# Two small unused tiles shift every SBUF pool of a one-core transformer layer

## The chip, the cores and the metric

The kernel runs on one core of a Trainium2 chip. The metric is the device time of one launch in microseconds; the kernel before has a median of 2428.5 us over three runs (2424.85, 2428.5 and 2429.57).

## The reference, cut to what matters

One layer of a hybrid backbone on 512 latent tokens (width 2048) with 256 context tokens in front of them, batch 1:

```
hx, hc = modulate(rms_norm(x)), modulate(rms_norm(ctx))      # scales and shifts from c @ w_mod, c_ctx @ w_mod
u, v, q, k, vv, g, d = split(hx @ w_in)                      # the same split of hc @ w_in for k, vv, d
a   = gelu(u) * (w_s @ layer_norm(gelu(v)) + b_s)            # chunks of 128 tokens, 8 heads
o   = gated linear attention of q, k, vv, d, forwards and backwards, starting from the context's state
y   = concat(a, norm(o) * silu(g)) @ w_out
x   = x + gate * rms_norm(y)
f   = (silu(h @ w_a) * (h @ w_b)) @ w_ffn_out                # h = modulate(rms_norm(x)), hidden width 5632
out = x + gate * rms_norm(f)
```

All inputs and the output are float32.

## The kernel before

**The products.** Each large product is built from TensorE matmuls of 128x128 weights against 512 streamed columns (256 for the context's keys). To keep float32 accuracy each operand is split in two float32r tiles: ScalarE copies the high part (`S.copy`), VectorE subtracts it from the source for the low part (`split`, L271; `parts`, L985). `three` (L295) then issues three matmuls for a pair, and L113 is the line of the helper `mm` that issues each:

```
        mm(o, a[0], b[0], start, False)
        mm(o, a[0], b[1], False, False)
        mm(o, a[1], b[0], False, stop)
```

The first operand is the stationary one (the weights that LDWEIGHTS puts in the array), the second the moving one, read column by column. The trace shows one LDWEIGHTS (PEld) for each matmul (PE). A small number of products (transposes by the identity, gate rows, the attention's small blocks) are in plain float32.

**The order.** Program order on each engine is the order of the code, fixed in advance. The stages are: the first modulation rows (`mb`), one third at a time of k, q and half of u (`k`, `q`, `u`), the rest of u and v (`u1a`, `v0a`, `v1a`), the context's keys and values (`ck` with its gate rows `cd`, then `cv`), the values and gates (`vv`, `g`) with the attention's small work threaded between, the output projection (`wo`), eleven groups of the FFN's input (`f0p` to `f10p`; each group computes 7 products of half size, 336 matmuls; `ffn_group`, L1133), the FFN's output in two halves (`fo`, L1241: 960 matmuls each) and its last four blocks of rows (`fz`, L1268: 192 matmuls). Weights come from DRAM through SyncE's queue in pieces of 512 KB.

**Where the tiles lie.** A tile pool takes a stretch of each partition's SBUF, from the left end upwards or (`side="right"`) from the right end downwards. A pool lies behind those that were opened before it. On the left stand, from byte 16512 of each partition: `cp` (constants and small vectors, 5856 bytes), `s2` (44 slots of 2 KB: the activations' split parts, called by `slot`), then `pp` with `sp`, `hcp` and `gl` one after the other, and later, in their place, `fp` (29 slots of 2 KB, by `fslot`). On the right stands `stg` (streamed weights, raw and split) and later, in its place, `st2` (the same for the second half of the kernel). The right end is at byte 229344.

Worked out from these sizes, the tiles of 2 KB of the left pools `s2`, `pp` and `fp` start at 2048 n + 1888, and the tiles of 2 and 4 KB of the right pools `stg` and `st2` at 2048 n + 2016. The context's tiles in `hcp` start at 2048 n + 864. Slices within a tile start at multiples of 512 bytes (128 columns of float32) further on, except for the gate rows' weights `wd`, whose slices step by 256 bytes. So, by the start modulo 512:

| matmuls | stationary operand | moving operand |
|---|---|---|
| `k`, `q`, `u`, `u1a`, `g` | right pool, 480 | `s2`, 352 |
| `v`, `vv`, `wo`, `f0p` to `f10p`, `fo` | `s2` or `fp`, 352 | right pool, 480 |
| `ck` | right pool, 480 | `hcp`, 352 |
| `cv` | `hcp`, 352 | right pool, 480 |
| `cd`, and `d` among `k` and `q` | `s2`, 352 and 96 in turn | `hcp` or `s2`, 352 |
| `fz` | `s2`, 352 | `s2` or `fp`, 352 |

All of these starts are 96 modulo 128.

Of the kernel before, what the change touches and what calls it, by code (L numbers as in the profile page):

```python
# [9 lines left out]
F32 = mybir.dt.float32  # L10
# [8 lines left out]
P = 128  # L19
# [72 lines left out]
def trunk_kernel(ctx, tc, cmat, cmask, x, c, ctxt, c_ctx, w_mod, b_mod, g_pre_mix, g_post_mix, g_pre_ffn,  # L92
# [4 lines left out]
    bg, bgm = Pump(), Pump()  # L97

    cp = ctx.enter_context(tc.tile_pool(name="cp", bufs=1))
    stg_ctx = ExitStack()  # L100
    stg = stg_ctx.enter_context(tc.tile_pool(name="stg", bufs=1, side="right"))
    s2 = ctx.enter_context(tc.tile_pool(name="s2", bufs=1))
# [1213 lines left out]
```

## Time and profile before

| | before |
|---|---|
| median of 3 runs | 2428.5 us |
| profiled execution | 2426.19 us, span 2424.4 us |
| PE busy (matmul) | 2319.1 us, 96% |
| PEld busy (weight load) | 1851.2 us, 76% |
| DVE / ACT / POOL busy | 1596.3 / 987.7 / 15.3 us |
| mean granted clock of TensorE | 0.979 |
| DMA | 470.99 MB, 194 GB/s over the span |

An engine's busy time is the time in which at least one of its instructions runs. Consecutive matmuls overlap in the records, so PE's busy share says only that it had work; how fast it goes is read from the starts of consecutive matmuls.

### The profile page before, as it was taken

To read this page: it belongs to the slowest core of one execution; us is meant where nothing else is said; L and a number is where in the kernel's file an instruction comes from. 1 tells how busy PE (TensorE), PEld (TensorE's weight loads), DVE (VectorE), ACT (ScalarE), POOL (GpSimd) and SP (SyncE) were. 2 spreads that over 40 slices of the span, in tenths; PEclk is the share of its full clock that TensorE was granted. 3 is DMA by queue.
4 is the path that set the end of the run, shared out by engine and by line. 5 is a ranking of instruction groups with operands and counts; after the bars stand their busy time and mean duration, and the time that the engine had idled before them with its cause. 6 is when DMAs were issued, how large, how long until landed. Compare 5 with 4: busy or idle time off the path is not lost.

```text
span 2424.4 us, 27761 instructions
## 1 busy us (share of the span) xinstructions
PE 2319.1 (96%) x10386; PEld 1851.2 (76%) x10386; DVE 1596.3 (66%) x2040; ACT 987.7 (41%) x1509; POOL 15.3 (1%) x22
## 2 busy tenths in 40 slices
PE   7999999999996989889999999999999899999998
PEld 2778888788885767658888778877787788888887
DVE  3876577677777777787778777877787632242246
ACT  4443234454564223854444444444344422241232
POOL 0000000000000000000000000000000000000000
PEclk9999998999997999899999999999999999999999
DMA  9957787734335989746567665765566542253344
GB/s 322 334 195 251 239 282 245 239 131 134 127 105 177 314 299 310 226 131 191 185 188 219 189 190 184 219 195 188 180 218 193 171 139 96 96 172 101 102 139 156
DMA packets 244134, 470.99 MB, mean 194 GB/s; under 512 B 20456, under 2 KB 31936, under 8 KB 244000
## 3 DMA queue, kind: packets, MB, share of 16 engines
q1 hardware_dynamic: 233280, 451.49, 57.6%
q10 hardware_dynamic: 10720, 17.74, 2.1%
q8 instruction: 81, 1.33, 0.2%
q14 instruction: 53, 0.43, 0.1%
HBM read 445.04 MB, written 24.13 MB: 194 GB/s over the span
## 4 chain that ended last, share of the span: by engine, by line
PE 81%; DMA 8%; DVE 6%; ACT 3%; issue 1%; SPq 0%; ACTq 0%; DVEq 0%
PE fo L113 19%; PE f7p L113 3%; PE f4p L113 3%; PE f9p L113 3%; PE f5p L113 3%; PE f1p L113 3%; PE f6p L113 3%; PE f3p L113 3%; PE f2p L113 3%; PE f10p L113 3%; PE f8p L113 2%; PE f0p L113 2%; PE v0a L113 2%; PE u1a L113 2%; PE g0a L113 2%; PE cv L113 2%
## 5 line engine op out<-in xcount | busy, mean ns | idle before, releaser
L1221 DVE TENSOR_TENSOR gl<-gr,gh 128x512 fp32r<-128x512 f32 x44 | 28.4, 687 | 24.2 <-ACT gh L1220 24.2
L1220 ACT CAST gh<-gr 128x512 fp32r<-128x512 f32 x44 | 25.1, 618 | 28.1 <-DMA gr<-g_dr 20.9
L226 DVE SCALAR_TENSOR_TENSOR m50acc<-m50w,cpair,m50acc 128x1024 f32<-128x1024 f32 x16 | 20.5, 1281 | 13.8 <-DMA m50w<-in_w_mod_dram 13.7
L990 DVE TENSOR_TENSOR fo_2l<-fo_r,fo_2h 128x1024 fp32r<-128x1024 f32 x8 | 9.8, 1226 | 29.6 <-ACT fo_2h L989 29.6
L829 ACT ACTIVATE lv<-lv 128x1024 f32<-128x1024 f32 x20 | 21.0, 1054 | 19.4 <-DVE lv L828 19.4
L990 DVE TENSOR_TENSOR fo_0l<-fo_r,fo_0h 128x1024 fp32r<-128x1024 f32 x8 | 9.8, 1225 | 28.3 <-ACT fo_0h L989 28.3
L113 PE MATMUL fo<-fo_0h,gh 128*128 128x512 f32 x64 | 26.4, 412 | 1.7 <-ACT gh L1220 1.7
L113 PE MATMUL vv0a<-vv_0h,hxh 128*128 128x512 f32 x64 | 27.7, 433 | 0.0
L990 DVE TENSOR_TENSOR fo_18l<-fo_r,fo_18h 128x1024 fp32r<-128x1024 f32 x8 | 9.8, 1225 | 27.1 <-ACT fo_18h L989 27.1
L990 DVE TENSOR_TENSOR fo_14l<-fo_r,fo_14h 128x1024 fp32r<-128x1024 f32 x8 | 9.8, 1225 | 26.3 <-ACT fo_14h L989 26.3
L113 PE MATMUL vv1a<-vv_0h,hxh 128*128 128x512 f32 x64 | 27.1, 424 | 0.0
L990 DVE TENSOR_TENSOR fo_12l<-fo_r,fo_12h 128x1024 fp32r<-128x1024 f32 x8 | 9.8, 1225 | 26.3 <-ACT fo_12h L989 26.3
L990 DVE TENSOR_TENSOR fo_10l<-fo_r,fo_10h 128x1024 fp32r<-128x1024 f32 x8 | 9.8, 1225 | 26.3 <-ACT fo_10h L989 26.3
L990 DVE TENSOR_TENSOR fo_16l<-fo_r,fo_16h 128x1024 fp32r<-128x1024 f32 x8 | 9.8, 1225 | 26.2 <-ACT fo_16h L989 26.2
L990 DVE TENSOR_TENSOR fo_8l<-fo_r,fo_8h 128x1024 fp32r<-128x1024 f32 x8 | 9.8, 1225 | 26.2 <-ACT fo_8h L989 26.2
L113 PE MATMUL g1a<-hxh,g_0h 128*128 128x512 f32 x64 | 26.6, 415 | 0.3 <-ACT g_0h L274 0.3
L113 PE MATMUL g0a<-hxh,g_0h 128*128 128x512 f32 x64 | 26.9, 420 | 0.0
L830 DVE TENSOR_TENSOR lv<-lv,kq 128x1024 f32<-128x1024 f32 x20 | 24.4, 1219 | 3.8 <-ACT lv L829 3.8
L113 PE MATMUL v1a<-v_0h,hxh 128*128 128x512 f32 x64 | 26.7, 417 | 0.0
L1280 ACT ACTIVATE junk<-fc 128x512 bf16<-128x512 f32 x16 | 10.1, 631 | 40.7 <-DVE fc L1279 40.6
L113 PEld LDWEIGHTS s<-lv 128*128 128x128 f32 x192 | 24.9, 191 | 2.0 <-issue 0.5
L113 PE MATMUL fo<-fo_0l,gh 128*128 128x512 f32 x64 | 26.0, 407 | 0.0
(3877 smaller groups left out, 8033.6 us busy)
## 6 DMA issues: line engine op xcount, KB each, us to landing
fo_r<-in_w_ffn_out_dram SPq DMA_DIRECT2D x80, 512.0 KB
gr<-g_dr SPq DMA_DIRECT2D x22, 512.0 KB
mx4w<-in_w_mod_dram SPq DMA_DIRECT2D x16, 512.0 KB
mx8w<-in_w_mod_dram SPq DMA_DIRECT2D x16, 512.0 KB
mx12w<-in_w_mod_dram SPq DMA_DIRECT2D x16, 512.0 KB
mc4w<-in_w_mod_dram SPq DMA_DIRECT2D x16, 512.0 KB
mc8w<-in_w_mod_dram SPq DMA_DIRECT2D x16, 512.0 KB
mc12w<-in_w_mod_dram SPq DMA_DIRECT2D x16, 512.0 KB
```

The lines of the kernel that those rows point to most:

```text
L113: return T.matmul(o, lhsT=l, rhs=r, start=start, stop=stop)
L226: ins = V.scalar_tensor_tensor(out=acc, in0=raw[:, j].rearrange("p i c -> p (i c)"), scalar=cvec[:, k0 + j:k0 + j + 1], in1=acc, op0=ALU.m ...
L829: S.activation(lv, lv, AF.Exp)
L830: V.tensor_tensor(out=lv, in0=lv, in1=kq[h], op=ALU.mult)
L990: V.tensor_tensor(out=wl, in0=src, in1=wh.bitcast(F32), op=ALU.subtract)
L1220: S.copy(hi, r[:, j * 512:(j + 1) * 512])
L1221: V.tensor_tensor(out=lo, in0=r[:, j * 512:(j + 1) * 512], in1=hi.bitcast(F32), op=ALU.subtract)
L1280: S.activation(junk, f, AF.Square, accum_out=fss[:, cg:cg + 1])
```

## The change

Two tiles are allocated and never used. `edge_l` (8 float32, 32 bytes of each partition) is the first tile of `cp` on the left, so everything on the left starts 32 bytes later. `edge_r` (24 float32, 96 bytes) stands in a pool of its own, opened on the right ahead of `stg`, so everything on the right starts 96 bytes earlier. No instruction is added, removed or moved.

```
     cp = ctx.enter_context(tc.tile_pool(name="cp", bufs=1))
+    edge = ctx.enter_context(tc.tile_pool(name="edge", bufs=1, side="right"))
+    edge.tile([P, 24], F32, name="edge_r")
+    cp.tile([P, 8], F32, name="edge_l")
     stg_ctx = ExitStack()
     stg = stg_ctx.enter_context(tc.tile_pool(name="stg", bufs=1, side="right"))
     s2 = ctx.enter_context(tc.tile_pool(name="s2", bufs=1))
```

After it, the tiles of `s2`, `pp` and `fp` start at 2048 n + 1920 and those of `stg` and `st2` too. Modulo 512 both columns of the table above read 384 (and the gate rows' weights 384 and 128), and every start in it is a multiple of 128. The constants' tile `mats` moves from a multiple of 128 to 32 past one.

## Rows read from the trace of the kernel before

**Rows 1.** The page: busy time by engine, and the chain that ended last.

```profile
PE 2319.1 (96%) x10386; PEld 1851.2 (76%) x10386; DVE 1596.3 (66%) x2040; ACT 987.7 (41%) x1509; POOL 15.3 (1%) x22
...
PE 81%; DMA 8%; DVE 6%; ACT 3%; issue 1%; SPq 0%; ACTq 0%; DVEq 0%
```

**Rows 2.** Windows by stage: busy us by engine, clock, DMA share, GB/s.

```profile
core 0: us, PE busy (x) PEld busy (x) DVE busy (x) ACT busy (x) POOL busy (x), PEclk, DMA share, GB/s
0.00:45.00 45.00, 29.66 (x77) 6.96 (x78) 13.31 (x66) 23.31 (x54) 3.81 (x10) 0.96 0.95 301
45.00:215.00 170.00, 165.16 (x743) 127.44 (x742) 124.83 (x189) 70.27 (x133) 0.96 (x1) 0.99 0.77 263
780.00:990.00 210.00, 194.28 (x801) 151.47 (x802) 152.04 (x152) 66.20 (x105) 2.87 (x3) 0.96 0.92 311
1107.00:1913.00 806.00, 803.46 (x3521) 645.46 (x3519) 621.12 (x621) 348.00 (x380) 0.00 (x0) 1.00 0.62 194
2149.00:2372.00 223.00, 223.00 (x962) 180.78 (x961) 78.04 (x85) 59.92 (x72) 0.00 (x0) 1.00 0.38 127
2372.00:2416.00 44.00, 43.71 (x193) 35.83 (x191) 30.82 (x60) 12.36 (x36) 0.00 (x0) 1.00 0.48 159
```

**Rows 3.** Who PE waited for in the FFN groups, 1107 to 1913 us.

```profile
PE f8p L113 <- DVE f8y2l L990: 0.4, 1, 0.4
PE f4T L1202 <- ACT f4t L1204: 0.2, 1, 0.2
```

**Rows 4.** Timeline of PE: first and last of the second half of `fo`.

```profile
2148.89 0.40 PE L113 MATMUL fo<-fo_0h,gh 128*128 128x512 f32 x1
...
2371.74 0.40 PE L113 MATMUL fo<-fo_18h,gl 128*128 128x512 f32 x1
```

**Rows 5.** Timeline of PE: the first, the 13th and the last of `fz`.

```profile
2371.98 0.40 PE L113 MATMUL fz<-flh,gh 128*128 128x512 f32 x1
...
2374.75 0.39 PE L113 MATMUL fz<-flh,gh 128*128 128x512 f32 x1
...
2415.33 0.39 PE L113 MATMUL fz<-flh,gl 128*128 128x512 f32 x1
```

**Rows 6.** Timeline of PE in `v0a`: first and last of 81 matmuls in a row.

```profile
286.23 0.40 PE L113 MATMUL v0a<-v_0l,hxh 128*128 128x512 f32 x1
...
304.90 0.40 PE L113 MATMUL v0a<-v_0h,hxh 128*128 128x512 f32 x1
```

**Rows 7.** Windows of PE around that stretch.

```profile
286.10:304.90 18.80, 18.80 (x82) 1.00 0.94 319
```

**Rows 8.** Timeline of PE in `u1a`: first and last of 131 matmuls in a row.

```profile
227.32 0.40 PE L113 MATMUL u1a<-hxh,u_0l 128*128 128x512 f32 x1
...
257.53 0.39 PE L113 MATMUL u1a<-hxh,u_0h 128*128 128x512 f32 x1
```

**Rows 9.** Timeline of PE: nine matmuls of `ck`, then nine of `cd`.

```profile
372.63 0.28 PE L113 MATMUL ck<-hch,ck_0h 128*128 128x256 f32 x1
...
373.69 0.28 PE L113 MATMUL cd<-hch,wdc 128*64 128x256 f32 x1
...
374.71 0.28 PE L113 MATMUL cd<-hcl,wdc 128*64 128x256 f32 x1
```

**Rows 10.** Plain float32 `mb0ps`: four records in a row, and all 32.

```profile
14.18 1.88 PE L113 MATMUL mb0ps<-mb0w,cpair 128*2 128x512 f32 x4 [0.86 <-DMA mb0w<-in_w_mod_dram]
...
L113 PE MATMUL mb0ps<-mb0w,cpair x32: 592/592/1061, 7.3 to 31.9; 128*2 128x512 f32 x32
```

**Rows 11.** VectorE's subtraction of `parts`: min, median and max ns of one.

```profile
L990 DVE TENSOR_TENSOR fo_2l<-fo_r,fo_2h x8: 1224/1226/1227, 1911.5 to 2311.9; 128x1024 fp32r<-128x1024 f32 x8
```

**Rows 12.** One FFN group (`f4p`): busy us by engine, clock, DMA share, GB/s.

```profile
1348.20:1428.80 80.60, 80.39 (x353) 64.41 (x352) 62.09 (x63) 34.83 (x38) 0.00 (x0) 1.00 0.63 196
```

**Rows 13.** The chain from 820 to 900 us (`wo`), by line.

```profile
by line: DMA m50w<-in_w_mod_dram 32.2%; DMA m21w<-in_w_mod_dram 14.7%; DVE m50acc L226 13.7%; DVE m21acc L226 12.4%; DMA m20g<-in_g_post_mix_dram 8.8%; DMA wo1r<-in_w_out_dram 7.4%; issue 5.7%; DVE yo L1029 5.4%; DVE wo14l L990 1.5%; DVE wo
```

More of the change, by code (lines that the diff above doesn't have):

```diff
@@ L99, in trunk_kernel @@
     cp = ctx.enter_context(tc.tile_pool(name="cp", bufs=1))
+    edge = ctx.enter_context(tc.tile_pool(name="edge", bufs=1, side="right"))
+    edge.tile([P, 24], F32, name="edge_r")
+    cp.tile([P, 8], F32, name="edge_l")
     stg_ctx = ExitStack()
```

## The prediction

> **What bounds the kernel now.** I read the page first: PE is busy for 96% of the span and the chain that ended last is 81% PE [rows 1]. The windows by stage then say where this holds [rows 2]. From 1107 to 1913 us (FFN groups) PE is busy 803.5 of 806 us, from 2149 to 2372 us (the second half of `fo`) 223 of 223, and in the FFN groups it waits for others only once for 0.4 us and some 0.2 us at a group's end, ten times [rows 3]. Two stretches are another's: before 45 us and from 780 to 990 us (`wo`) the DMA engines are busy 95% and 92% at 301 and 311 GB/s, and in `wo` the chain runs over the loads of `w_mod` and VectorE's sums of them, not over PE [rows 2, 13]. So a faster matmul shortens everything but those two, and nothing else on the chip does much.
>
> A busy PE says nothing of its pace, so the next view is the timeline of PE, start to start. The second half of `fo` has 960 matmuls of 512 columns: from the first start to the last, 222.85 us over 959 steps, 232.4 ns each [rows 4]. In `fz` the 13th to the last of 192 take 40.58 us over 179 steps: 226.7 ns each [rows 5]; its first twelve take 2.77 us, 230.8 ns each, so the faster pace is reached within 3 us of the change of operands. In `v0a` it is 18.67 us over 80 steps, 233.4 ns [rows 6], in `u1a` 30.21 us over 130 steps, 232.4 ns [rows 8]. These are three steady paces for the same instruction with the same shape. At 2.4 GHz (granted clock 1.00 in the windows of `fz`, `fo` and `v0a` [rows 2, 7]) they are 544, 558 and 560 cycles for 512 columns.
>
> What differs between `fz` and the rest? Not the other engines: VectorE is busy 70% in `fz` and 35% in the `fo` stretch, DMA 0.48 against 0.38, so the faster pace stands beside the busier neighbours; `v0a` has DMA at 0.94 and is only 1 ns slower than `fo` [rows 2, 7]. It is the layout: `fz` is the only stage in which both operands' starts agree modulo 512 (352 and 352); in all others with 512 columns they lie 128 bytes apart (352 and 480; the gate rows `d`, 32 single matmuls among those of `k` and `q`, aside). The 256-column matmuls give a second pair: nine steps of `ck` (480 against 352) take 1.06 us, 117.8 ns each, and the nine steps of `cd` behind them (352 or 96 against 352) 1.02 us, 113.3 ns each [rows 9]. I read this as: weight load and moving stream disturb each other when their starts differ by 128 modulo 256, less or not at all when they agree.
>
> **The change, part by part.** No instruction comes or goes. Every left pool moves by +32, every right pool by -96 bytes. Pools on one side keep their order and distances; between the sides the distance falls by 128 bytes. `fp` ended at 171872 and `st2` began at 172000; both edges are now 171904, so nothing new overlaps, and `st2` lies over the same tiles of `gl` and `hcp` as before. So I take waits and order as unchanged: 0 us.
>
> *The pace of matmuls.* After the change all pairs of the table agree modulo 512, as only `fz` and half of `cd` did. If agreement is the cause, 232.4 becomes 226.7: 5.7 ns each. Term by term:
> - `fo`: 2 x 960 x 5.7 = 10.9 us. PE is alone there: DMA 0.38, VectorE 35% [rows 2].
> - FFN: 11 groups x 336 x 5.7 = 21.1 us, 1.9 us a group. One group takes 80.6 us with VectorE busy 62.1 us and ScalarE 34.8 [rows 12]; at 78.7 us VectorE still has 16.6 us to spare, so PE stays the bound.
> - `u1a`, `v0a`, `v1a`, `cv`, `vv` and `g` (two each): 8 x 192 = 1536 matmuls x 5.7 = 8.8 us, taken at the smaller gain.
> - `ck`: 192 x (117.8 - 113.3) = 0.9 us.
> - `k`, `q`, `u` in 45 to 215 us: 608 x 5.7 = 3.5 us. DMA is at 0.77 and 263 GB/s, PE busy 165 of 170 us [rows 2]; I take half, 1.7 us.
> - `wo`: 768 x 5.7 = 4.4 us of PE's work, counted at nothing, since DMA and VectorE's sums set the end [rows 13]; if they did not, it would be 4.4 us more.
> - `fz`: already there, 0.
>
> Sum 43.4 us. What is late next: in `fo` nothing; in the FFN VectorE, but only if a group fell towards 62 us.
>
> *What the trace can't show.* No float32r operand before starts at a multiple of 128, so the bounds are these. From below (a gain): the plain float32 records show four in a row in 1.88 us; less the last one's 592 ns that is 429 ns a step [rows 10], 1030 cycles for 512 columns, that is almost exactly two cycles a column. So the extra 32 cycles of 544 are no fixed cost of a matmul, and could go with the alignment: the best pace is half of 429, 214.5 ns. From above (a loss): 560 cycles plus as much again as divides `fz` from `v0a`, 576 cycles or 240 ns. I take 226.7, the row whose starts agree.
>
> *VectorE, ScalarE, DMA.* VectorE's subtraction spreads by 3 ns around 1226 [rows 11]; were it 5% slower, a group's 62.1 us became 65.2, still covered. DMA writes to all these tiles start at 96 modulo 128 before, so no row shows another alignment; 2% either way on the 255 us of the DMA-bound stretches [rows 2] is 5 us, which I keep for the range and take as 0. `mats`, now 32 past a multiple of 128, is read only by short matmuls: no cost taken.
>
> The profiled execution is 2426.2 us (span 2424.4), 2.3 us under the median of 2428.5. 2426.2 - 43.4 = 2382.8; against the median, 2385.
>
> Here a rule speaks against the change. The Trainium skill, "TensorE: Matmul & The Clock Gate", Part 2, Step-by-step, says that weight loads and the moving operand have separate SBUF read ports and that loading the next weights takes nothing from the running matmul. By it the starts would not matter and the sum would be 0, the first rival below; rows 5 and 9 don't agree with it as far as the layout, and not the stage, is what sets the two paces apart.
>
> **The rivals.**
> 1. *The pace of `fz` is due to something else*: its weights and its stream both lie in left pools (in every other stage one of the two is in a right pool), or its twelve matmuls in a row for one bank. For it: the trace can't part this from the starts, since the same matmuls have both. Against it: `u1a` streams from the left with weights from the right, `fo` the other way round, both at 232.4 [rows 4, 8], so it would have to be any tile on the right, on whichever of the two reads. Then nothing changes: 2428, within 5 us.
> 2. *The alignment gives more*: 214.5 ns [rows 10]. Then `fo` gains 1920 x 17.9 = 34.4, `fz` 2.3, the FFN up to 66.2 (a group of 74.6 us, with VectorE at 83% and some waits at the products' ends), the eight blocks 27.5, the rest some 7: 137 us of PE time, of which I let a sixth get lost in new waits. 2428.5 - 115 = 2313. For it: 544 is 17/16 of 512, and 272 cycles for 256 columns in `cd` (113.3 ns) too, so the loss goes with the columns read. Against it: no row shows it at full speed. The Trainium skill, "TensorE: Matmul & The Clock Gate", Back-to-back issue gap, has 215.7 ns for 512 columns as a measured gap of one isolated stream; by that figure the sum would be about this rival's. No run here shows it.
> 3. *Slower: agreement at a multiple of 128 makes the two reads collide each time.* Weight load and stream now begin at the same place of the same kind of line. Place: every float32r matmul. Price: 240 ns, 7.6 ns more on 1920 + 3696 + 1536 + 304 = 7456 matmuls, 57 us: 2485. It decides from 233.1 ns a step on (5 us over 7456 matmuls). For it: nothing says that the starts of `fz` are good at another alignment. Against it: in `fz` the quarter of the matmuls whose weights are the first slice of their tile start at the same residue modulo 2048 as the stream, and keep 226.7 [rows 5]. A milder form is the pace of `v0a` everywhere, 233.4: 2435.
> 4. *Half of it*: the pace falls in some stages only, since the patterns depend on how a stage begins (`v0a` and `fo` differ by 1 ns with the same starts). 2400 to 2420.
>
> **How the numbers follow.** Forecast (226.7 nearly everywhere) 0.45, rival 2 0.18, rival 4 0.07, rival 1 0.18, rival 3 0.12. A run of this kernel tells about 0.2% (5 us) from no change. Faster: 0.45 + 0.18 + 0.07 = 0.70; the same: 0.18; slower: 0.12. The forecast's own range is 2372 to 2400 (the 4.4 us of `wo`, the DMA's 5 us, and a third of the FFN's gain lost to waits). The range must leave out no more than 0.2: it goes up to 2433 (rival 1 whole, and 3 left out but for its mildest form) and down to 2315 (about half of rival 2). That leaves out about 0.2.
>
> **What would show it.** In `fo` after: 960 matmuls from first to last start in 217.4 us (226.7) for the forecast, 222.9 for rival 1, 205.7 for rival 2, 230 for rival 3. `fz`: 226.7 as before, except in rivals 2 and 3. One FFN group: 78.7 us against 80.6. `ck`: 113 to 114 ns. `wo`, 210 us from 780 to 990, should stay within 3 us. The forecast is wrong if `fo` keeps 232 ns while its operands agree, or if the groups of the FFN shorten by less than PE's steps do, with new waits of PE for VectorE's `parts`.

## The result, and the profile after

The kernel after takes 2391.5 us (median of four runs, 2387.5 to 2393.6) against 2426.7 for the kernel before on the same chip (four runs, 2419.4 to 2429.6): ratio 0.986, interval 0.983 to 0.988, 35 us. The prediction was 2385.

The profiled execution of after took 2393.61 us, with a span of 2391.8. Every engine has as many instructions as before, and the granted clock is 0.979 in both. The page of after, busy time by engine and the chain that ended last; these answer to [rows 1]:

```profile
PE 2279.7 (95%) x10386; PEld 1843.2 (77%) x10386; DVE 1595.1 (67%) x2040; ACT 987.8 (41%) x1509; POOL 15.3 (1%) x22
...
PE 64%; DVE 15%; DMA 14%; issue 3%; ACT 3%; SPq 0%; DVEq 0%; ACTq 0%
```

PE's busy time fell by 39.4 us, but the span only by 32.6, and the chain says where to look: PE has 64% of it instead of 81, VectorE and the DMA together 29% instead of 14. Something that PE used to cover now shows.

Windows of after at its own stage bounds (`k` to `u`, `wo`, the FFN groups f1 to f10, the second half of `fo`), columns as in [rows 2]:

```profile
44.40:211.40 167.00, 161.82 (x742) 127.04 (x742) 123.68 (x187) 69.10 (x131) 0.96 (x1) 0.99 0.78 266
767.40:980.50 213.10, 196.55 (x802) 155.15 (x803) 152.77 (x152) 65.78 (x104) 2.86 (x3) 0.93 0.90 307
1095.10:1891.30 796.20, 790.76 (x3521) 642.80 (x3520) 619.80 (x621) 348.32 (x380) 0.00 (x0) 1.00 0.62 196
2121.60:2339.10 217.50, 217.50 (x961) 180.10 (x960) 77.91 (x85) 60.30 (x73) 0.00 (x0) 1.00 0.40 130
```

The FFN window has the same 3521 matmul records as the one of before in 796.2 us instead of 806, and in it PE is without work for 5.4 us instead of 2.5 [rows 2]. The second half of `fo` is still PE without a gap. The timeline of PE in after: first and last matmul of that half, then the 13th and the last of `fz`:

```profile
2121.52 0.39 PE L116 MATMUL fo<-fo_0h,gh 128*128 128x512 f32 x1
...
2338.89 0.39 PE L116 MATMUL fo<-fo_18h,gl 128*128 128x512 f32 x1
...
2341.84 0.39 PE L116 MATMUL fz<-flh,gh 128*128 128x512 f32 x1
...
2382.41 0.39 PE L116 MATMUL fz<-flh,gl 128*128 128x512 f32 x1
```

`fo`: 217.37 us over 959 steps, 226.7 ns, where [rows 4] had 232.4. `fz`: 40.57 us over 179 steps, 226.6, as in [rows 5]. Who PE waits for in the FFN groups of after, answering to [rows 3] (total us, times, longest):

```profile
PE f1p L116 <- DVE f1e0l L993: 1.0, 1, 1.0
PE f9p L116 <- DVE f9e0l L993: 0.9, 1, 0.9
PE f1p L116 <- DVE f1b1l L993: 0.8, 1, 0.8
PE f10p L116 <- DVE f10e0l L993: 0.5, 1, 0.5
```

These are waits for VectorE's low parts, which [rows 3] had once. Lined up by the starts of their stages, the two profiled executions differ like this (us gained, each rounded; the last row is the difference of the spans):

| stretch | predicted | measured |
|---|---|---|
| ahead of `k` | 0 | 1.2 |
| `k`, `q`, `u` | 1.7 | 2.2 |
| `u1a`, `v0a`, `v1a`, `cv`, `vv`, `g` | 8.8 | 7.4 |
| `ck` | 0.9 | 2.4 |
| `wo` | 0 | -3.6 |
| FFN, f0 | 1.9 | 2.1 |
| FFN, f1 to f10 | 19.2 | 9.8 |
| `fo` | 10.9 | 11.2 |
| `fz` and the end | 0 | -0.3 |
| sum | 43.4 | 32.6 |

Two questions come out of it: is it really the agreement of the starts, and where are the nearly ten microseconds that the FFN is short of?

### The profile page after: what moved, and what is told of

It is laid out like the page before. It is cut to its first block, busy times and chain, and to the rows that moved or that the text cites. A ratio compares the mean times of both kernels' runs of the same rounds, so it can differ in the third digit from the quotient of the medians.

```text
span 2391.8 us, 27761 instructions
## 1 busy us (share of the span) xinstructions
PE 2279.7 (95%) x10386; PEld 1843.2 (77%) x10386; DVE 1595.1 (67%) x2040; ACT 987.8 (41%) x1509; POOL 15.3 (1%) x22
## 4 chain that ended last, share of the span: by engine, by line
PE 64%; DVE 15%; DMA 14%; issue 3%; ACT 3%; SPq 0%; DVEq 0%; ACTq 0%
PE fo L116 18%; PE f7p L116 3%; PE f8p L116 3%; PE f5p L116 3%; PE f4p L116 3%; PE f0p L116 2%; PE g0a L116 2%; PE u1a L116 2%; PE fz L116 2%; PE vv1a L116 2%; PE cv L116 2%; PE wo L116 2%; PE f2p L116 2%; PE k L116 2%; PE v1a L116 2%
## 5 line engine op out<-in xcount | busy, mean ns | idle before, releaser
L229 DVE SCALAR_TENSOR_TENSOR m51acc<-m51w,cpair,m51acc 128x1024 f32<-128x1024 f32 x16 | 20.5, 1283 | 8.5 <-DMA m51w<-in_w_mod_dram 8.2
```

The costliest lines, as they stand in the source:

```text
L229: ins = V.scalar_tensor_tensor(out=acc, in0=raw[:, j].rearrange("p i c -> p (i c)"), scalar=cvec[:, k0 + j:k0 + j + 1], in1=acc, op0=ALU.m ...
```

## Experiments on the pace: what about the starts matters

**Agreement alone.** The kernel before with one unused tile of 128 bytes on the left. Left and right now agree modulo 2048, but at 2016, which is 96 modulo 128 as before.

```
+    cp.tile([P, 32], F32, name="edge_l")
```

> The left pools move by 128 bytes (one unused tile of 32 float32 at the head of cp), the right ones not at all: all 2 KB tiles start at 2016 modulo 2048, so the operands agree, but every start is 96 past a multiple of 128, as before. Theory A, agreement of the two starts sets the pace: fo steps of 226.7 ns, its second half in 217.5 us, time 2385 to 2397, as with the change. Theory B, the multiple of 128 does it: 232.4 ns, 222.9 us, 2420 to 2432.

**Alignment alone.** The kernel after with one buffer of the small tile `mv` instead of two, which takes 128 bytes from the left: every start is a multiple of 128, the two sides 128 apart.

```
-        mv = cp.tile([P, NT, 4, 2], F32, tag="mv", bufs=2, name=f"mv{g}")
+        mv = cp.tile([P, NT, 4, 2], F32, tag="mv", bufs=1, name=f"mv{g}")
```

> The change with one small pair of cp tiles (mv of the gating, 128 bytes each) held once and not twice: the left 2 KB tiles start at 1792 modulo 2048, the right ones at 1920. All start at multiples of 128, but the two operands lie 128 apart again. Theory A (agreement): fo steps of 232.4 ns, second half 222.9 us, fz 226.7 ns, time 2420 to 2432. Theory B (alignment): fo steps of 226.7 ns, 217.5 us, 2385 to 2397. The gating's second group may wait for its first: under 3 us by either.

Measured: agreement alone 2396.0 us, ratio to before 0.987 (0.985 to 0.990); alignment alone 2422.6 us, ratio 0.998 (0.996 to 0.999). First and last matmul of the second half of `fo`, with agreement alone:

```profile
2126.43 0.39 PE L114 MATMUL fo<-fo_0h,gh 128*128 128x512 f32 x1
...
2343.80 0.39 PE L114 MATMUL fo<-fo_18h,gl 128*128 128x512 f32 x1
```

and with alignment alone:

```profile
2146.47 0.40 PE L116 MATMUL fo<-fo_0h,gh 128*128 128x512 f32 x1
...
2369.32 0.40 PE L116 MATMUL fo<-fo_18h,gl 128*128 128x512 f32 x1
```

217.37 us (226.7 ns) against 222.85 (232.4). Agreement gives the whole pace without any alignment, and alignment gives nothing to it. The 5 us by which alignment alone still is below before (2428.0 us on that chip) are not in the pace: its `wo` starts 7.1 us earlier than before's although its steps up to there take 232 to 233 ns as well, and `wo` then gives most of it back (214.0 us instead of 209.3). What moves the stages ahead of `wo` by some microseconds from kernel to kernel stays open.

**Which distances.** Edges of 64, 96 and 32 bytes on the left of the kernel before bring the sides 64, 32 and 96 bytes apart (left below right); one buffer of `mv`, alone or with the edge of 64 bytes, makes it 256 and 192.

```
+    cp.tile([P, 16], F32, name="edge_l")     # 64 apart; P, 24: 32 apart; P, 8: 96 apart
```

> Left pools moved by 64 bytes alone: the operands' starts lie 64 apart (1952 and 2016 modulo 2048). Theory A in its strict form, any disagreement disturbs: fo steps between 230 and 240 ns, time 2420 or more. Theory A with a threshold, only a distance of 128 in 256 disturbs: 226.7 ns, 2385 to 2397. Theory B (alignment): no start is a multiple of 128 (left 32, right 96 past one), so 232.4 ns or more.

> Left pools moved by 96 bytes alone: the operands' starts lie 32 apart (1984 and 2016 modulo 2048). Strict agreement: fo steps between 230 and 240 ns. Threshold: 226.7 ns. Alignment (left 64, right 96 past a multiple of 128): 232.4 ns or more.

> The kernel before with a left edge of 32 bytes: left 1920, right 2016 modulo 2048, 96 bytes apart. Known are 0 apart (226.7 ns), 32 apart (233.3 and 233.2), 64 apart (228.9 in fo, 233.3 in u1a), 128 apart (232.4). A theory of distance in steps of 32 bytes expects fo and u1a between 228.9 and 233.3 ns and not 226.7. A theory by which only multiples of 64 are kind, by alignment, expects 233.3 in both. Whole: 2412 to 2428 us.

> The kernel before with one buffer of mv and a left edge of 64 bytes: left 1824, right 2016 modulo 2048, 192 bytes apart. In the kernel 64 bytes apart, fo (stationary 64 below moving) had 228.9 ns and u1a (stationary 64 above) 233.3. Theory A, a signed distance modulo 256: 192 below is 64 above, so the two change places, fo 233.3 and u1a 228.9 ns. Theory B, the plain distance up to 2048: fo and u1a both 232 to 234 ns, nothing changes places. Whole: 2405 to 2420 us by A, 2425 by B.

> The kernel before with one buffer instead of two for the small tile mv: left pools start 128 bytes lower, so the starts of stationary and moving tile are 256 bytes apart in fo, u1a and the like (left 1760, right 2016 modulo 2048). Theory A, the pace depends on the distance modulo 256: every stage takes 226.7 ns, fo's second half 217.4 us, the whole 2396 us, as with agreement alone. Theory B, only full agreement (modulo 512 or more) helps: fo 231 to 234 ns, 222 to 224 us, the whole 2420 to 2428 us. fz is 226.7 by both. Theory C, ck's 256-column step depends on the start of its stationary tile alone and not on the distance: it stays between 117 and 120 ns.

One run each: 2407.3 us (64), 2426.5 (32), 2431.6 (96), 2429.1 (192), 2389.2 (256). Timeline of PE in the kernel 64 apart: first and last of a stretch of `u1a` (161 matmuls, weights from the right, stream from the left), then of the second half of `fo` (weights from the left, stream from the right):

```profile
224.04 0.39 PE L114 MATMUL u1a<-hxl,u_0h 128*128 128x512 f32 x1
...
261.36 0.40 PE L114 MATMUL u1a<-hxh,u_0l 128*128 128x512 f32 x1
...
2133.49 0.39 PE L114 MATMUL fo<-fo_0h,gh 128*128 128x512 f32 x1
...
2353.00 0.39 PE L114 MATMUL fo<-fo_18h,gl 128*128 128x512 f32 x1
```

The same rows of the kernel 192 apart:

```profile
220.25 0.39 PE L114 MATMUL u1a<-hxl,u_0h 128*128 128x512 f32 x1
...
256.88 0.39 PE L114 MATMUL u1a<-hxh,u_0l 128*128 128x512 f32 x1
...
2150.99 0.39 PE L114 MATMUL fo<-fo_0h,gh 128*128 128x512 f32 x1
...
2374.76 0.39 PE L114 MATMUL fo<-fo_18h,gl 128*128 128x512 f32 x1
```

64 apart: `u1a` 37.32 us over 160 steps, 233.3 ns, and `fo` 219.51 over 959, 228.9. At 192 the two change places: `u1a` 36.63 us, 228.9 ns, `fo` 223.77, 233.3. That is what a distance counted from the weights' start to the stream's, modulo 256, makes of them, and no theory of either side alone does. The second half of `fo` in the kernel 256 apart closes the ring:

```profile
2117.46 0.39 PE L113 MATMUL fo<-fo_0h,gh 128*128 128x512 f32 x1
...
2334.83 0.39 PE L113 MATMUL fo<-fo_18h,gl 128*128 128x512 f32 x1
```

217.37 us, 226.7 ns, though modulo 512 the starts don't agree there. In all of these kernels `fz`, whose operands both lie on the left, keeps 226.7 ns.

At 96 apart, the same two stretches again:

```profile
224.40 0.40 PE L114 MATMUL u1a<-hxl,u_0h 128*128 128x512 f32 x1
...
261.88 0.39 PE L114 MATMUL u1a<-hxh,u_0l 128*128 128x512 f32 x1
...
2153.41 0.39 PE L114 MATMUL fo<-fo_0h,gh 128*128 128x512 f32 x1
...
2377.18 0.39 PE L114 MATMUL fo<-fo_18h,gl 128*128 128x512 f32 x1
```

`u1a` takes 234.3 ns a step and `fo` 233.3. At 32 apart both take 233.3.

Several expectations missed. At 64 neither the strict theory (230 to 240 ns in `fo`) nor the one with a threshold (226.7) had 228.9. Of the whole times, 192 apart took 2429.1 us where theory A had 2405 to 2420, 96 apart 2431.6 where 2412 to 2428 was written, and 256 apart 2389.2 where theory A had 2396. And `ck` did not come as expected: its steps behind each other take about 119.3 ns at 0, 128 and 256 apart alike, 114.0 in the kernel 64 apart, and 116.8 to 118.2 in the others. The theory written ahead, that its weights' start decides alone, is not borne out either; `ck` stays open.

## Experiments on the FFN: where half of its gain went

First the account, from start to start in the records of f1 to f10, up to the first transpose behind f10. Steps of 200 to 250 ns (the shorter steps of the transposes aside): 3282 of 232.6 ns on average before, 3244 of 227.0 after, so the pace gives back its 18 us. The steps of 250 ns and more, counted above 227 ns, sum to 14.4 us before and 23.1 after: 8.7 us are new, and they stand ahead of few tiles, above all the parts `e0` (from 0.0 to 5.0 us, high and low part together) and `b1` (from 0 to 4.3 us). VectorE's timeline in after at the start of group f3 shows how `b1l` comes late (the bracket is its idle time, and what ended it):

```profile
1263.51 1.22 DVE L993 TENSOR_TENSOR f3b0l<-f3b,f3b0h 128x1024 fp32r<-128x1024 f32 x1
1269.61 1.23 DVE L1169 TENSOR_TENSOR f3X<-f3X,f3c 128x1024 f32<-128x1024 f32 x1 [4.89 <-DMA f3c<-in_w_ffn_in_dram]
1270.75 1.22 DVE L993 TENSOR_TENSOR f3b1l<-f3b,f3b1h 128x1024 fp32r<-128x1024 f32 x1
```

The section on the kernel before says that program order on each engine is the order of the code. Here it is not: in the source all four additions `X += c` stand behind `b3l`, but in the program as built the first of them stands ahead of `b1l`, in all ten groups of before and of after. The load of `c` can be issued only when `b0l` has freed a raw buffer, and SyncE's queue waits for just that:

```profile
SPq L195 <- DVE f3b0l L993: 14.4, 1, 14.4
```

So VectorE stands there for 4.89 us, with `b1l` behind it though `b1`'s data is there. PE at that place:

```profile
1271.55 0.39 PE L116 MATMUL f3p<-f3b1h,S2h 128*128 128x512 f32 x1
1272.02 0.50 PE L116 MATMUL f3p<-f3b1l,S2h 128*128 128x512 f32 x1
```

`b1l` ends at 1271.97, the matmul that reads it starts at 1272.02, 0.47 us behind its forerunner instead of 0.23. The kernel before had the same stand of VectorE, 4.45 us long; its timeline there, VectorE first and then PE:

```profile
1281.33 1.23 DVE L1166 TENSOR_TENSOR f3X<-f3X,f3c 128x1024 f32<-128x1024 f32 x1 [4.45 <-DMA f3c<-in_w_ffn_in_dram]
1282.47 1.22 DVE L990 TENSOR_TENSOR f3b1l<-f3b,f3b1h 128x1024 fp32r<-128x1024 f32 x1
```

```profile
1284.03 0.39 PE L113 MATMUL f3p<-f3b1h,S2h 128*128 128x512 f32 x1
1284.26 0.40 PE L113 MATMUL f3p<-f3b1l,S2h 128*128 128x512 f32 x1
```

There `b1l` ended at 1283.69, 0.57 us ahead of its matmul: hidden, by half a microsecond. In the ten groups this lead was 0.3 to 0.7 us; in after every one of the ten matmuls follows its `b1l` at once, by 0.05 or 0.06 us. Two things used the lead up. Counted from the group's first matmul and averaged over the ten groups, PE would be at this place 0.27 us earlier in after, and `b1l` ends 0.54 us later (16.49 instead of 15.95 us), most of it because VectorE stands longer for the load: 4.94 us on average instead of 4.49. PE's faster steps are thus the smaller part. Why the load lands later no run here shows; agreement alone and the kernel 256 apart, which have the fast pace too, stand 4.88 and 4.95 us.

**One more raw buffer.** The obvious cure, an earlier load: five raw buffers instead of four, paid for with two preloaded tiles.

```
-NF = 29
+NF = 27
...
-        return st2.tile([P, 1024], F32, tag="R", bufs=4, name=name)
+        return st2.tile([P, 1024], F32, tag="R", bufs=5, name=name)
```

> The kernel after with five raw buffers R instead of four and 27 instead of 29 preloaded tiles, the memory for the fifth. It tells why the ten FFN groups f1 to f10 gave back only about 10 us of 19. Theory D: VectorE stands in order behind the loads f#c, which SyncE can issue only when a raw buffer comes free, and so writes the last parts late; with a fifth buffer the loads come earlier, a group falls to about 78.7 us, f1 to f10 take 786 to 790 us instead of 796, the whole 2381 to 2386 us, ratio to the kernel before 0.981 to 0.984. Theory E: VectorE, not the loads, is too slow in the end of a group: f1 to f10 stay at 794 to 798 us and the whole at 2389 to 2395 us, ratio 0.985 to 0.987. If two tiles fewer in advance delay the first groups, f0 grows by some us, which would hide part of D.

2394.0 us, ratio to before 0.987 (0.985 to 0.989). The whole is where theory E had it, but f1 to f10 took 801.4 us, more than either theory had, while f0 took 108.1 instead of 114.4. VectorE's timeline at the same place:

```profile
1260.24 1.22 DVE L1169 TENSOR_TENSOR f3X<-f3X,f3c 128x1024 f32<-128x1024 f32 x1
1265.26 1.23 DVE L1169 TENSOR_TENSOR f3X<-f3X,f3c 128x1024 f32<-128x1024 f32 x1 [3.80 <-DMA f3c<-in_w_ffn_in_dram]
1266.40 1.22 DVE L993 TENSOR_TENSOR f3b1l<-f3b,f3b1h 128x1024 fp32r<-128x1024 f32 x1
```

The load is earlier, but the order of the program as built moved with it: the first addition now stands ahead of `a1l`, and the third ahead of `b1l`, where VectorE waits 3.80 us for its load. So the run did not take the suspect away; it left open whether the order or VectorE's amount of work was to blame.

**The order alone.** The kernel after, with the additions `X += c` put behind `b3l` on VectorE. Nothing else is touched in the source.

```
-        V.tensor_tensor(out=wl, in0=src, in1=wh.bitcast(F32), op=ALU.subtract)
+        low[0] = V.tensor_tensor(out=wl, in0=src, in1=wh.bitcast(F32), op=ALU.subtract).ins
...
+        b_low = low[0]                       # behind the loop over product 2
...
-            V.tensor_tensor(out=X[q], in0=X[q], in1=r, op=ALU.add)
+            with tc.issue_after(b_low):      # product 5 only
+                V.tensor_tensor(out=X[q], in0=X[q], in1=r, op=ALU.add)
```

> The kernel after, with the four additions X += c of each FFN group put behind b3l on VectorE, so that VectorE no longer stands 4.9 us before the load f#c with b1l to b3l behind it. It is to tell why f1 to f10 gave back about 10 of 19 us. Theory D (VectorE's order in front of the late load makes the parts late): the steps of PE over 250 ns, 23.1 us above 227 in after, fall to about 14 to 16 us, those before f#b1l and f#e0l (9.2 us with their high halves) nearly vanish, f1 to f10 take 786 to 790 us instead of 796, the whole 2381 to 2386 us. Theory E (VectorE has too much to do before e0l, whatever the order): b1l's 3 us go, e0l's 5 us stay or grow, f1 to f10 790 to 795 us, the whole 2386 to 2391 us.

The same with five raw buffers and 27 preloaded tiles:

> The same with five raw buffers and 27 preloaded tiles instead of four and 29. In five_raw the additions stood even earlier in VectorE's order (before a1l) and f1 to f10 took 801 us. Theory D: with the additions behind b3l the earlier loads help, f1 to f10 785 to 789 us, the whole 2380 to 2386 us, at or below the kernel with four buffers. Theory F (five buffers with two preloaded tiles fewer cost by themselves, the order has no part in it): f1 to f10 stay at 797 to 802 us, the whole 2391 to 2396 us.

And on the kernel before, as a control:

> The control: the kernel before, with the same additions put behind b3l. PE takes 232.4 ns a step there and the FFN groups hardly wait, so by theory D the order is hidden: f1 to f10 804 to 806 us, the whole 2421 to 2428 us, ratio 0.998 to 1.001. If the reorder gives 5 us or more here too (ratio below 0.998), its gain in the kernel after has nothing to do with the faster pace.

The six kernels (each ratio is to runs of before on the same chip; f1 to f10 from the first to the last matmul):

| kernel | us | ratio to before | f1 to f10 | steps of 250 ns and more, above 227 |
|---|---|---|---|---|
| before | 2424.9 | 1 | 805.8 us | 14.4 us |
| before, additions behind | 2424.4 | 1.000 (0.998 to 1.001) | 804.6 | 13.1 |
| after | 2391.5 | 0.986 (0.983 to 0.988) | 795.9 | 23.1 |
| after, five raw buffers | 2394.0 | 0.987 (0.985 to 0.989) | 801.4 | 29.7 |
| after, additions behind | 2383.3 | 0.983 (0.981 to 0.985) | 785.4 | 13.1 |
| after, both | 2385.2 | 0.983 (0.981 to 0.985) | 785.5 | 13.1 |

VectorE's timeline of the kernel after with the additions behind, in f3:

```profile
1261.87 1.23 DVE L993 TENSOR_TENSOR f3b0l<-f3b,f3b0h 128x1024 fp32r<-128x1024 f32 x1
1265.74 1.23 DVE L993 TENSOR_TENSOR f3b1l<-f3b,f3b1h 128x1024 fp32r<-128x1024 f32 x1 [2.65 <-ACT f3b1h L992]
...
1272.33 3.49 DVE L1173 TENSOR_TENSOR f3X<-f3X,f3c 128x1024 f32<-128x1024 f32 x3
```

`b1l` now ends 3.2 us ahead of its matmul, which starts at 1270.13, and the three additions run without a pause since their loads have landed. The chain of waits from 1500 to 1600 us in that kernel is PE alone:

```profile
by line: PE f6p L116 68.5%; PE f7p L116 29.8%; PE f6T L1209 2.0%; issue 0.0%
```

The program as built changed in more places than the source: other additions on VectorE slid as well. One of these moves bears on `e0`. In after (and before) the addition `y += z` stands ahead of the last `X += e` and of `e0l`, and it too waits for a load. The chain of after in f1 (start, us, what):

```profile
1134.25 5.65 DMA f1y<-in_w_ffn_in_dram
...
1139.99 0.06 DVE f1y L1191
...
1141.13 1.22 DVE f1X L1182
1142.35 1.14 DVE f1e0l L993
```

With the additions behind, `e0l` comes first, in all ten groups and in the control as well. VectorE's timeline there in f1:

```profile
1139.28 1.22 DVE L993 TENSOR_TENSOR f1e0l<-f1X,f1e0h 128x1024 fp32r<-128x1024 f32 x1
1140.41 1.22 DVE L1195 TENSOR_TENSOR f1y<-f1y,f1z 128x1024 f32<-128x1024 f32 x1
```

So the run tests these moves together, that of `c`'s additions from ahead of `b1l` and that of `y`'s from ahead of `e0l`; no run makes one without the other.

Theory D holds, for VectorE's order as a whole: the waits ahead of `b1` and of `e0` are both gone, a group takes 78.6 us where the prediction had 78.7, and the reorder is worth nothing that could be told from no change in the kernel before (control). Theory E falls, as VectorE does the same work. Theory F falls too: with the order mended five buffers cost nothing in f1 to f10, and they bring nothing either. On the whole time, against the kernel before, the additions behind bring 0.983 where after has 0.986. The two intervals overlap by a little, so the whole times alone do not part the two; in the stretch that was edited the gain is 10.5 us of 796.

## Why the prediction was right, and where not

- *PE bounds nearly all of it, and its pace is read start to start.* Right: in after the median step is 227 or 228 ns in every stage of float32r matmuls with 512 columns, and `fo`, where PE has no gaps, gained 11.2 us where the term had 10.9. So rival 4 (only some stages) falls.
- *Agreement of the starts is the cause.* Right, and shown: agreement alone does it, alignment alone does not. Rival 1 (the sides, or twelve matmuls in a row for one bank) falls with agreement alone, which leaves every tile on its side and every matmul in its place. Rivals 2 and 3 fall with the kernel after itself: at multiples of 128 a step is neither 214.5 nor 240 ns but 226.7. "Modulo 512" was too narrow: 256 is enough.
- *Weight loads beside the stream.* By the Trainium skill, "TensorE: Matmul & The Clock Gate", Part 2, Step-by-step, loading weights takes nothing from the running matmul, and nothing would have changed. The runs differ from what would follow: the same instructions took 226.7 to 234.3 ns a step by where the two operands start, so the measurement decides. That it is the weight load and the stream that disturb each other is the prediction's reading; no run here leaves the weight loads out, and what in the hardware makes the step depend on the starts stays open. The 215.7 ns that the prediction cites with rival 2 stand on the same page of the Trainium skill, in Step-by-step and not under the heading that it names; no stage of float32r matmuls here has a steady pace under 226.7 ns.
- *`cd` as a second witness.* Wrong. After the change `ck` keeps its 119.3 ns (117.8 in the nine steps of [rows 9]) and `cd` its 114.4, with the starts in agreement. The two differ in the width of the weights as well, 128 and 64 columns, and the prediction put the difference down to the starts. The stage did get 2.4 us shorter, but not by its steps: the granted clock around it was 0.93 before and 0.96 in after, which may be why. `fz` alone carried the argument. The two windows, before and after:

```profile
366.00:461.00 95.00, 89.01 (x498) 77.79 (x498) 64.25 (x120) 40.39 (x80) 2.03 (x3) 0.93 0.76 250
...
359.00:452.00 93.00, 86.33 (x509) 76.19 (x509) 65.63 (x124) 41.67 (x82) 2.65 (x3) 0.96 0.78 260
```

- *FFN 21.1 us.* The mis-sized term: it measured 11.9. The step that failed is "at 78.7 us VectorE still has 16.6 us to spare, so PE stays the bound". The 16.6 us were there, but partly spent in places where VectorE can do nothing else, behind an addition that waits for its load. What counted was how far `b1l` and `e0l` were ahead of their matmuls, 0.57 us for `b1l` in f3, not the sum of idle time. With that order mended f1 to f10 give back 20.4 us, a little over the 19.2 that the term had for them.
- *`wo` 0.* It came out 3.6 us longer, past the 3 us that the prediction allowed it. Over all the kernels here it took 209 to 214 us with no tie to the pace (214.0 with the old pace in the kernel with alignment alone, 210.9 with the new one 256 apart), so it is no price of the change that could be shown. The granted clock in its window was 0.96 before [rows 2] and 0.93 in after, so part of the 3.6 us may be the clock. The same caution holds for the small terms ahead of it.
- *Waits and order unchanged.* The order was; the waits were not. One of the two marks by which the prediction would call itself wrong, groups that shorten by less than PE's steps do, with new waits of PE for VectorE's `parts`, is what was seen: the forecast holds for the pace and fails for the FFN's waits. Part of the nearness of 2391.5 to 2385 is luck: 1.2 us ahead of `k` and 1.5 us more than the term of `ck`, neither from the pace, make up for most of what `wo` lost.

## What to carry to other kernels

Where a matmul's steady step is a few per cent over another stage's with the same shape and clock, compare where the stationary and the moving tile start within 256 bytes of a partition; an unused tile of some bytes in one pool may be all it takes. Before counting a gain on the bounding engine in full, look for each neighbour's order, in the trace and not in the source: an instruction that waits for a load with ready work behind it has no slack to give, whatever its engine's idle share. And when an added buffer doesn't help, see first whether the order of the program as built moved with it.

## What was not expected of the hardware

The step of a float32r matmul with its own weight load, 128x512 at a granted clock of 1.00, by the distance from the weights' start up to the stream's start, modulo 256 bytes. A kernel that is called 64 apart above has 64 in `fo` (weights left, stream right) and 256 - 64 = 192 in `u1a` (the other way round). The columns 0 to 128 are read from `fo`, 160 and 224 from `u1a` (96 and 32 apart), 192 from both:

| distance | 0 | 32 | 64 | 96 | 128 | 160 | 192 | 224 |
|---|---|---|---|---|---|---|---|---|
| ns a step | 226.7 | 233.3 | 228.9 | 233.3 | 232.4 | 234.3 | 233.3 and 233.3 | 233.3 |
| cycles at 2.4 GHz | 544 | 560 | 549 | 560 | 558 | 562 | 560 | 560 |

Zero is best, 64 next, and the ring is not symmetric: 64 is quick and 192 is not. For `ck`, with 256 columns, another of these distances is the quickest of the six that it had: 114.0 ns at 192, but 119.3 at 0. At 128 there are two paces for the same starts: 232.4 in `fo` of the kernel before, 233.3 in `fo` of the control with the additions behind, and in `v0a` [rows 6]; what chooses between them is open. No run reached half of the plain float32 step (214.5 ns): 32 cycles over the 512 columns remain at the best distance too.
